# Start addresses of the linear layers' operands set to multiples of 2048 bytes

## The chip, the cores and the metric

The kernel runs on one core of one Trainium2 chip. The metric is the device time of one execution in microseconds (us), the median of several runs. TensorE does the matrix products; VectorE (DVE), ScalarE (ACT) and GpSimd (POOL) do the rest out of the same on-chip memory, SBUF; SyncE (SP) issues the transfers from DRAM. SBUF has 128 partitions; a tile takes the same byte range of each, and "start" below means the byte of a partition at which an operand begins.

## The reference

512 tokens of 1024 features go through two blocks of two layers each, in float32.

```python
def first_block(x, ...):
    h = x
    for layer in range(2):
        hn = _rmsnorm(h, norm_mix[layer])
        h = h + attention(hn) @ w_o          # layer 0: stick-breaking, layer 1: dilated with rotary
        h = h + _swiglu(_rmsnorm(h, norm_ffn[layer]), w_gate[layer], w_up[layer], w_down[layer])
    return _rmsnorm(h, norm_final)

def second_block(x, ...):
    h = x
    for layer in range(2):
        mix = hgrn2_mixer(h, ...) if layer == 0 else swa_sink_mixer(h, ...)
        h = layer_norm(ALPHA * h + mix, ...)
        ff = conv_ffn(h, ...)                # up-projection, causal convolution of 3 taps, SiLU gate, down
        h = layer_norm(ALPHA * h + ff, ...)
    return h
```

Each attention has 16 heads of 64 features, or 8 of 128 in the recurrence `hgrn2_mixer`; each feed-forward has 2816 hidden features.

## The kernel before

Activations lie with their features on the partitions and the 512 tokens along them. A float32 matrix product is carried by three products of the type float32r: each operand is split into a first part (its value rounded) and a second part (the rest), and `mm3` multiplies first by first, second by first and first by second into the same PSUM bank. The three products that recur everywhere are thus `xh` with `whi`, `xh` with `wlo`, and `xl` with `whi`; in a profile's `bank<-xh,whi` the two names are the two operands in the order of the trace, first the streamed one (moving), then the one that is loaded into the array (stationary, a weight tile of 128x128, 512 bytes of a partition).

Weights come in blocks of 512 KB (`w_dma`), are split by ScalarE (`w_hi`) and VectorE (`w_lo`) into one of three pairs of rooms `whi0/wlo0` to `whi2/wlo2` (a fourth pair from the second block on), and are used by

- `cols`: 128 output features by all 512 tokens, the weights stationary, the activations moving, 512 columns (2048 bytes) at a time. Nearly all products have this form. `cols_n`, `half_unit` and `late_unit` are variants, the last two also by halves of 256 tokens, around the second block's layer norms.
- `rows`: four tiles of tokens by 256 features for the attentions' values, with the activations stationary and the weights moving, 256 columns (1024 bytes) at a time.

The moving activations are `xh`/`xl` (normed layer input, `[128, 8, 512]`, held for the whole program in the pool `fix`), `hh`/`hl` (hidden features of a feed-forward) and `oh`/`ol` (output of an attention). The last two pairs lie in pools that are opened and closed by layer, the rows of one are 2048 bytes apart, so that all eight have the same start modulo 2048.

Four stretches are woven: the products of an attention's projections alternate by hand-written shares (`weave`) with the attention itself, whose steps wait for VectorE and ScalarE. Between them the feed-forwards run products alone. The order of all engines' instructions is the order of the Python program; no scheduler changes it.

Where a tile lies is decided by the pools alone: `fix`, `ring`, `tmp` and the layer's pool stand behind one another, and within a pool tiles stand in the order in which they are first asked for, each rounded up to 32 bytes. In `fix` the first is `vecs` with 1924 bytes, so that what follows starts off every larger multiple. The starts that come of it, modulo 2048:

| tile | used as | before | after |
|---|---|---|---|
| `x`, `xh`, `xl` | moving (and stationary in `rows`) | 544 | 0 |
| `whi0`..`wlo3`, staging `wst` | stationary (and moving in `rows`) | 1888, so 1888, 352, 864, 1376 by weight tile | 0, so 0, 512, 1024, 1536 |
| `hh`, `hl` of the first block; `oh`, `ol` of the first block | moving | 1888 | 0 |
| `hh`, `hl` and `oh`, `ol` of the second block | moving | 1504 | 0 |
| `sph`, `spl` (stick-breaking, moving) | moving | 1888 and 864 | 0 and 1024 |
| `ntri`, `nones` (stick-breaking) | stationary | 352, 864 | 512, 1024 |
| `acc`, `r_bc`, `dg` | sums and factors of the norms | 1632, 1632, 1664 | 0 |

Of the kernel before, what the change touches and what calls it, by code (L numbers as in the profile page):

```python
# [8 lines left out]
F32 = mybir.dt.float32  # L9
# [7 lines left out]
P = 128  # L17
S = 512
# [8 lines left out]
# the first two weight blocks come by halves, between the tiles of x  # L27
# [6 lines left out]
# ---------------------------------------------------------------- weight order  # L34
def plan():
    """The weight tiles in the order in which the tensor engine takes them: a
    block is (matrix, [(row tile, column tile), ...], gain vector or None)."""
    out = []
# [58 lines left out]
# ------------------------------------------------------------ per-feature rows  # L97
# [25 lines left out]
def _shape_constants():  # L123
# [6 lines left out]
    i = np.arange(P)  # L130
# [16 lines left out]
    # relative position buckets: column u stands for the distance 255 - u  # L147
# [52 lines left out]
# ------------------------------------------------------------------ the program  # L200
# [9 lines left out]
class Prog:  # L210
# [3 lines left out]
    # -- small helpers  # L214
    def defer(self, f):
        """f waits for another engine: its engine takes other work first."""
        self.pend.append(f)
# [9 lines left out]
    def warm(self, n):  # L227
        """keeps the tensor engine's clock up while it waits."""
        for _ in range(n):
            self.mm(self.bank[0][:, 0:P], self.ones, self.ones, True)  # L230
# [9 lines left out]
    # -- weight stream: DRAM -> stage -> (hi, lo) parts in float32r  # L240
# [8 lines left out]
    def w_part(self, i, c):  # L249
        """the split of a part of a block."""  # L250
        if i not in self.split:
            self.split[i] = self.rooms.pop(0)
        st, (hi, lo) = self.staged[i][:, c], self.split[i]
        self.nc.scalar.activation(out=hi[:, c], in_=st, func=AF.Copy)
        self.nc.vector.tensor_tensor(out=lo[:, c], in0=st, in1=hi[:, c].bitcast(F32), op=ALU.subtract)

    def w_gain(self, i):
        """the gains of the blocks up to the i-th."""
# [11 lines left out]
    def w_room(self, pool, n):  # L270
        """room for one more split block."""
        self.rooms.append((pool.tile([P, 1024], F32R, name=f"whi{n}", bufs=1), pool.tile([P, 1024], F32R, name=f"wlo{n}", bufs=1)))

    def w_hi(self):
        """the first parts of the next block."""
# [32 lines left out]
    def w_free(self, n=1):  # L308
        """the oldest n blocks are used."""
# [3 lines left out]
    def w_done(self, n, evac):  # L313
        """the oldest n blocks are used: evac, and the split of the blocks that take their room."""
# [7 lines left out]
    # -- products: three float32r passes carry a float32 product  # L322
# [5 lines left out]
    def cols(self, name, ks, rhs, bank, evac, grain=4, then=None):  # L328
        """bank[128 features, S] (+)= W[ks, tile].T @ act; a generator of pieces."""
# [11 lines left out]
    def cols_n(self, names, ks, rhs, banks, evacs, mid=None):  # L341
        """column tiles at once, k by k, for inputs that are still being made."""
# [10 lines left out]
    def first_cols(self, names, rhs, banks, evacs, scaled=None, ready=None, late=False):  # L353
        """a phase's first three column tiles, evacuated once r_bc is made."""
# [21 lines left out]
    def rows(self, name, lhs, banks, evac, grain=16):  # L376
        """four token tiles [128 tokens, 256 features] = act.T @ W, two of them to a bank."""
# [23 lines left out]
    def half_unit(self, blk, rhs, bank, own=False):  # L401
        """k-th products of a column tile for a half of the tokens; the halves share the bank, or own one each."""
# [51 lines left out]
    def weave(self, lin, n_lin, side, n_side, lead=0, first=0):  # L454
        """the n_lin pieces of `lin`, each with its share of the n_side pieces of `side`."""
# [13 lines left out]
    # -- scores q.k of 64 features: two passes carry the three products  # L469
    def pair_tiles(self, pool, o, p):  # L470
        """operands of a pair of heads: [k first; k second], [q first; q first] of each, and q second of both;
        a third of the pairs has them where the last pairs' outputs will be."""
# [9 lines left out]
    def pair_k(self, t, src, eng=None):  # L482
        """the parts of k: the first where its head lies, the second in the other half of the partitions."""
# [16 lines left out]
    def scores(self, out, t, h, lhs, ks, qs, start):  # L500
        """out = q.k of a head, the operand `lhs` ("k" or "q") stationary."""
# [5 lines left out]
    # -- norms  # L507
    def split_act(self, dst, j, src, gain=None):
        """dst (hi, lo)[:, j] = src * gain in two float32r parts."""
# [19 lines left out]
    def rms_prep(self, m, gain):  # L529
        """x[m] is final: its part of the mean square, and its two-part product operand."""  # L530
# [3 lines left out]
    def rsqrt(self, y, v, t):  # L534
        """y = v ** -0.5 for v > 0: a first guess from the exponent's bits, three Newton steps."""
# [12 lines left out]
    def rms_stats(self):  # L548
        """r_tok[token, tile] and r_bc[*, token] = (mean square + 1e-6) ** -0.5"""
# [16 lines left out]
    def ln_shift(self, m, banks):  # L566
        """less the mean of x[0] over its features, which a layer norm doesn't see."""
# [8 lines left out]
    def ln_add(self, m, bank, cs=slice(0, S), direct=False):  # L576
        """x[m] is complete with what `bank` adds, and enters the sums of x and of its square."""
# [18 lines left out]
    def ln_stats(self, hf):  # L596
        """the factors of the tokens of a half; a generator of its small steps."""
# [32 lines left out]
    def ln_apply(self, hf):  # L630
        """x = LN(x) of a half of the tokens, and its two-part product operand; a generator of pieces."""
# [35 lines left out]
    def layer_norm(self, units, frees, g, b, split=True, table=None):  # L667
        """the last products before a layer norm, by halves of the tokens: the norm of the first
        half goes on beside the products of the second. `frees`: units whose block is used up then."""
# [39 lines left out]
    def bridge(self, units, third, done, fill=()):  # L709
        """the first products after a layer norm, by halves of the tokens, beside the norm of the second half."""  # L710
# [67 lines left out]
    # -- set-up  # L778
    def setup(self):
# [4 lines left out]
        for i in range(3):  # L784
            self.w_room(self.ring, i)
# [4 lines left out]
        self.ident = f.tile([P, P], F32, name="ident")  # L790
        self.x = f.tile([P, KT, S], F32, name="x")
        self.xn = (f.tile([P, KT, S], F32R, name="xh"), f.tile([P, KT, S], F32R, name="xl"))
        nc.scalar.dma_start(out=self.vecs, in_=A["vecs"])
# [7 lines left out]
        self.ones = f.tile([P, P], F32, name="ones")  # L801
        nc.vector.memset(self.ones, 1.0)
        self.mean_w = f.tile([P, P], F32, name="mean_w")
        nc.vector.memset(self.mean_w, 1.0 / P)
        self.avg = f.tile([P, 2], F32, name="avg")
        nc.vector.memset(self.avg, 1.0 / 1024)
        self.eps6 = f.tile([P, 1], F32, name="eps6")
        nc.vector.memset(self.eps6, 1e-6)
        self.acc = f.tile([P, S], F32, name="acc")
        self.r_bc = f.tile([P, S], F32, name="r_bc")  # L810
        self.r_tok = f.tile([P, 4], F32, name="r_tok")
        self.dg = f.tile([P, 4, P], F32, name="dg")
        self.small = f.tile([P, 8], F32, name="small")

    def setup2(self):
        nc, f = self.nc, self.fix
        # lower bound: first row of the softmax over the two rows of logits
        self.lb = f.tile([P, 16], F32, name="lb")
        t = f.tile([P, 32], F32, name="lbt")
# [11 lines left out]
    def rel_setup(self):  # L831
        """what makes DRAM rows of every head's bias by distance: 128 equal rows each, to be read sheared."""
# [8 lines left out]
        self.hot = f.tile([33, 384], F32, name="hot")  # L841
        self.nc.vector.memset(self.rel, 1.0)
# [12 lines left out]
    # -- first block, layer 0: stick-breaking attention  # L855
    def stick(self):
        nc = self.nc
        lin, zr = Ring(self.bank[0:2] + self.bank[7:]), Ring(self.bank[2:6])
        with self.tc.tile_pool(name="stick", bufs=1) as pool:
# [74 lines left out]
            def s1b(p, u):  # L934
                W, off, banks = UW[u], UOFF[u], st[p, u]
                for h, e in enumerate(st.pop((p, u, "e"))):
# [7 lines left out]
                    # a block of keys and all later ones, for the blocks of keys before it  # L944
# [59 lines left out]
    # -- gated feed-forward of the first block  # L1004
# [43 lines left out]
    # -- first block, layer 1: dilated attention, its branches as one softmax  # L1048
    def dilated(self):
# [3 lines left out]
        with self.tc.tile_pool(name="dil", bufs=1) as pool:  # L1053
# [12 lines left out]
            def tick(n=1):  # L1066
                """what waits for a rope, some pieces later."""
# [61 lines left out]
            # block (keys j, queries i) of the weights lies at i + 3 j for the first head of a pair, 7 + 3 i + j for the second  # L1129
# [555 lines left out]
```

## Time and profile before

| | |
|---|---|
| median of 3 runs | 2611.56 us |
| lowest and highest | 2609.57, 2617.84 us |
| span of the profiled execution | 2614.2 us |
| TensorE busy | 2568.6 us (98%) |
| VectorE, ScalarE, GpSimd busy | 60%, 40%, 17% |
| granted clock of TensorE, mean | 0.988 |

The span of the profiled execution is itself 2.6 us over the median of the runs and inside their range. In the profile a matmul's duration is longer than the distance to the next one's start, since matmuls overlap in the array; where they follow one another without a wait, the distance from start to start is what one costs.

### The profile page before, as it was taken

Reading aid. Unit: us, or ns where it says so; the run is one execution under the profiler, and the core shown is the slowest. Engines: PE = TensorE matmul, PEld = TensorE weight load, DVE = VectorE, ACT = ScalarE, POOL = GpSimd, SP = SyncE. Lnnn points to the kernel's source line nnn. Section 1 sums busy time; section 2 is a strip of 40 time slices with the busy share of each in tenths; the row PEclk is TensorE's granted clock in tenths of the full one; section 3 lists DMA queues with packets and bytes.
Section 4 is the critical chain, followed back from the end, with each engine's and each line's share of the span. In section 5 each row is a group of like instructions: output and inputs, shape, how many; then the busy total and the mean of one; then the engine's idle time right before and its main releaser. Section 6 shows DMA issues by size and latency. Waiting matters only on the chain.

```text
span 2614.2 us, 32942 instructions
## 1 busy us (share of the span) xinstructions
PE 2568.6 (98%) x12732; PEld 2093.9 (80%) x12732; DVE 1556.6 (60%) x2580; ACT 1045.7 (40%) x1736; POOL 443.7 (17%) x394
## 2 busy tenths in 40 slices
PE   9999999999999999999999999999999999999998
PEld 7777888888767778888888888788788777888787
DVE  7665643444767654344476667754556788745556
ACT  6666422223445442222333333533333574523243
POOL 2111100001545210000111124100102325000103
PEclk9999999999999999999999999999999999999999
DMA  4111222222322122322221112232222312222221
GB/s 144 56 42 49 89 97 97 86 100 97 98 64 77 63 92 89 105 89 97 97 93 58 64 41 73 92 110 89 89 96 82 105 49 81 89 97 87 99 92 54
DMA packets 71277, 220.19 MB, mean 84 GB/s; under 512 B 8741, under 2 KB 15013, under 8 KB 71120
## 3 DMA queue, kind: packets, MB, share of 16 engines
q1 hardware_dynamic: 70512, 216.57, 24.3%
q8 instruction: 100, 1.64, 0.3%
q0 software_dynamic: 464, 1.27, 0.2%
q14 instruction: 57, 0.47, 0.1%
q10 hardware_dynamic: 144, 0.25, 0.0%
HBM read 209.14 MB, written 5.24 MB: 82 GB/s over the span
## 4 chain that ended last, share of the span: by engine, by line
PE 89%; DVE 8%; ACT 2%; issue 1%; DMA 0%; SPq 0%; POOL 0%; ACTq 0%; DVEq 0%
PE bank L225 88%; DVE wlo L295 1%; DVE lt L640 1%; DVE pr L1544 1%; PE bank L1161 1%; ACT whi L286 1%; DVE pr L1531 0%; DVE ln_sm L545 0%; DVE hg L1261 0%; DVE pr L1153 0%; PE bank L1554 0%; DVE xl L653 0%; DVE hq L1338 0%; DVE sm L1534 0%; DMA x<-in_xT 0%
## 5 line engine op out<-in xcount | busy, mean ns | idle before, releaser
L286 ACT ACTIVATE whi<-wst 128x1024 fp32r<-128x1024 f32 (+2 forms) x410 | 411.1, 1008 | 974.4 <-PE bank L225 781.9
L225 PE MATMUL bank<-xh,whi 128*128 128x512 f32 (+1 forms) x1992 | 788.6, 396 | 6.9 <-DVE xh L650 4.8
L225 PE MATMUL bank<-xl,whi 128*128 128x512 f32 (+1 forms) x1992 | 781.5, 392 | 4.9 <-DVE xl L653 2.6
L225 PE MATMUL bank<-xh,wlo 128*128 128x512 f32 (+1 forms) x1992 | 779.1, 391 | 1.4 <-DVE wlo L295 1.3
L295 DVE TENSOR_TENSOR wlo<-wst,whi 128x1024 fp32r<-128x1024 f32 (+2 forms) x392 | 485.3, 1243 | 100.4 <-ACT whi L286 97.4
L225 PEld LDWEIGHTS bank<-xh,whi 128*128 128x128 f32 x1992 | 378.7, 190 | 100.6 <-issue 14.7
L225 PEld LDWEIGHTS bank<-xl,whi 128*128 128x128 f32 x1992 | 378.2, 190 | 96.7 <-DVE xl L653 7.1
L225 PEld LDWEIGHTS bank<-xh,wlo 128*128 128x128 f32 x1992 | 378.8, 190 | 83.0 <-DVE wlo L295 2.3
L225 PE MATMUL bank<-hh,whi 128*128 128x512 f32 (+1 forms) x760 | 286.9, 378 | 0.0
L225 PE MATMUL bank<-hh,wlo 128*128 128x512 f32 (+1 forms) x760 | 285.9, 376 | 0.0
L225 PE MATMUL bank<-hl,whi 128*128 128x512 f32 (+1 forms) x760 | 285.6, 376 | 0.0
L527 POOL TENSOR_TENSOR acc<-acc,sq 128x512 f32<-128x512 f32 x35 | 49.9, 1427 | 803.4 <-ACT sq L526 803.0
L770 DVE TENSOR_TENSOR x<-x,bank 128x512 f32<-128x512 f32 x96 | 66.0, 688 | 190.7 <-PE bank L225 190.6
L225 PEld LDWEIGHTS bank<-hh,wlo 128*128 128x128 f32 x760 | 143.1, 188 | 27.3 <-issue 0.5
L225 PEld LDWEIGHTS bank<-hh,whi 128*128 128x128 f32 x760 | 143.0, 188 | 27.3 <-issue 0.5
L225 PEld LDWEIGHTS bank<-hl,whi 128*128 128x128 f32 x760 | 143.1, 188 | 26.8
L574 POOL TENSOR_TENSOR x<-x,r_bc 128x512 f32<-128x512 f32 x32 | 46.7, 1466 | 492.4 <-ACT r_bc L572 430.6
L225 PE MATMUL bank<-whi,xh 128*128 128x256 f32 x416 | 121.1, 291 | 0.0
L1406 DVE SCALAR_TENSOR_TENSOR b<-bank,vecs,b 128x511 f32<-128x511 f32 x88 | 65.9, 749 | 92.3 <-ACT b L1404 90.7
L1406 DVE SCALAR_TENSOR_TENSOR a<-bank,vecs,a 128x511 f32<-128x511 f32 x88 | 65.9, 749 | 90.2 <-ACT a L1404 88.7
L225 PE MATMUL bank<-whi,xl 128*128 128x256 f32 x416 | 118.3, 284 | 0.0
L225 PE MATMUL bank<-wlo,xh 128*128 128x256 f32 x416 | 118.1, 284 | 0.0
(285 smaller groups left out, 3536.6 us busy)
## 6 DMA issues: line engine op xcount, KB each, us to landing
wst<-in_w SPq DMA_DIRECT2D x314, 512.0 KB, 3.2
wst<-in_w SPq DMA_DIRECT2D x64, 448.0 KB, 3.1
wst<-in_w SPq DMA_DIRECT2D x36, 256.0 KB, 2.6
t<-t SPq DMA_DIRECT2D x56, 64.0 KB, 2.0
rel_scratch<-sq SPq DMA_DIRECT2D x16, 192.0 KB, 2.0
x<-in_xT SPq DMA_DIRECT2D x8, 256.0 KB, 6.1
bias<-rel_scratch SPq DMA_DIRECT2D x16, 128.0 KB, 2.8
out_dram<-x SPq DMA_DIRECT2D x16, 128.0 KB, 1.8
```

Source lines behind the costliest of these rows:

```text
L225: self.nc.tensor.matmul(out, lhsT=l, rhs=r, start=start, stop=True, skip_group_check=True)
L286: self.nc.scalar.activation(out=self.split[i][0][:, 0:n], in_=self.staged[i][:, 0:n], func=AF.Copy)
L295: (eng or self.lo_eng or self.nc.vector).tensor_tensor(out=lo[:, 0:n], in0=st[:, 0:n], in1=hi[:, 0:n].bitcast(F32), op=ALU.subtract)
L527: self.defer(lambda: eng.tensor_tensor(out=self.acc, in0=self.acc, in1=sq, op=ALU.add))
L574: nc.gpsimd.tensor_tensor(out=self.x[:, j, :], in0=self.x[:, j, :], in1=self.r_bc, op=ALU.subtract)
L640: nc.vector.scalar_tensor_tensor(out=t, in0=self.x[:, m, cs], scalar=gm, in1=self.acc[:, cs], op0=ALU.mult, op1=ALU.mult)
L770: self.nc.vector.tensor_tensor(out=self.x[:, m, :], in0=self.x[:, m, :], in1=bank, op=ALU.add)
L1161: nc.tensor.transpose(bk[:, P * j:P * j + P], pr[h][:, P * j:P * j + P], self.ident)
L1406: nc.vector.scalar_tensor_tensor(out=t[:, sh:S], in0=bank[:, 0:S - sh], scalar=self.vec(f"cw{l}{tap}", f), in1=t[:, sh:S], op0=ALU.mult, o ...
L1544: nc.vector.tensor_scalar(out=pr[h][:, 0:W], in0=pr[h][:, 0:W], scalar1=sm[:, 4 + h:5 + h], scalar2=None, op0=ALU.mult)
```

## The change

No instruction is added, taken away, or put elsewhere in any engine's order, and none gets another shape. Tiles get other starts: in `setup` the small tiles (`ident`, `ones`, `mean_w`, `avg`, `eps6`, `r_tok`, `small`, `lb`, `lbt`) are allocated first, then 160 bytes of padding (`pad`), which bring the pool to a multiple of 2048; behind them `x`, `xh`, `xl`, `acc`, `r_bc`, `dg` and the weight rooms, all of whole multiples of 2048 bytes. In `rel_setup` a padding of 384 bytes (`pad2`) does the same for the pool `fix2`, behind which the layers' pools of the second block begin. Everything moves up by 160 bytes or, in `fix2` and behind, by up to 544. Comments were dropped as well.

```diff
     def setup(self):
...
-        for i in range(3):
-            self.w_room(self.ring, i)
...
         self.ident = f.tile([P, P], F32, name="ident")
+        self.ones = f.tile([P, P], F32, name="ones")
+        self.mean_w = f.tile([P, P], F32, name="mean_w")
+        self.avg = f.tile([P, 2], F32, name="avg")
+        self.eps6 = f.tile([P, 1], F32, name="eps6")
+        self.r_tok = f.tile([P, 4], F32, name="r_tok")
+        self.small = f.tile([P, 8], F32, name="small")
+        self.lb = f.tile([P, 16], F32, name="lb")
+        self.lbt = f.tile([P, 32], F32, name="lbt")
+
+        f.tile([P, 40], F32, name="pad")
         self.x = f.tile([P, KT, S], F32, name="x")
         self.xn = (f.tile([P, KT, S], F32R, name="xh"), f.tile([P, KT, S], F32R, name="xl"))
+        self.acc = f.tile([P, S], F32, name="acc")
+        self.r_bc = f.tile([P, S], F32, name="r_bc")
+        self.dg = f.tile([P, 4, P], F32, name="dg")
+        for i in range(3):
+            self.w_room(self.ring, i)
...
-        self.ones = f.tile([P, P], F32, name="ones")
         nc.vector.memset(self.ones, 1.0)
-        self.mean_w = f.tile([P, P], F32, name="mean_w")
...
-        self.acc = f.tile([P, S], F32, name="acc")
-        self.r_bc = f.tile([P, S], F32, name="r_bc")
-        self.r_tok = f.tile([P, 4], F32, name="r_tok")
-        self.dg = f.tile([P, 4, P], F32, name="dg")
-        self.small = f.tile([P, 8], F32, name="small")
...
     def rel_setup(self):
...
         self.hot = f.tile([33, 384], F32, name="hot")
+        f.tile([P, 96], F32, name="pad2")
```

## Rows read from the trace of the kernel before

**Rows 1.** The page's first parts: busy us (share of span) by engine; granted clock.

```profile
span 2614.2 us, 32942 instructions
...
PE 2568.6 (98%) x12732; PEld 2093.9 (80%) x12732; DVE 1556.6 (60%) x2580; ACT 1045.7 (40%) x1736; POOL 443.7 (17%) x394
...
PEclk9999999999999999999999999999999999999999
```

**Rows 2.** The page's chain that ended last, by line.

```profile
PE bank L225 88%; DVE wlo L295 1%; DVE lt L640 1%; DVE pr L1544 1%; PE bank L1161 1%; ACT whi L286 1%; DVE pr L1531 0%; DVE ln_sm L545 0%; DVE hg L1261 0%; DVE pr L1153 0%; PE bank L1554 0%; DVE xl L653 0%; DVE hq L1338 0%; DVE sm L1534 0%; DMA x<-in_xT 0%
```

**Rows 3.** Groups by form, TensorE: names, shapes, xcount | busy us, mean ns | idle before.

```profile
L225 PE MATMUL bank<-xh,whi 128*128 128x512 f32 x1880 | 751.5, 400 | 1.3 <-ACT xh L516 0.9 <-DVE x L770 0.3
...
L225 PE MATMUL bank<-hh,whi 128*128 128x512 f32 x648 | 254.8, 393 | 0.0
...
L225 PE MATMUL bank<-whi,xh 128*128 128x256 f32 x416 | 121.1, 291 | 0.0
...
L225 PE MATMUL bank<-oh,whi 128*128 128x512 f32 x208 | 84.6, 407 | 0.1
...
L225 PE MATMUL bank<-hh,whi 128*128 128x256 f32 x112 | 32.1, 286 | 0.0
...
L225 PE MATMUL bank<-oh,whi 128*128 128x256 f32 x96 | 27.5, 286 | 0.0
```

**Rows 4.** Timeline, TensorE, 550 to 590: start us, duration us, instruction; 173 rows.

```profile
549.74 0.39 PE L225 MATMUL bank<-xl,whi 128*128 128x512 f32 x1
...
589.87 0.40 PE L225 MATMUL bank<-xh,whi 128*128 128x512 f32 x1
```

**Rows 5.** The same, 510 to 545 us, first block's feed-forward; 156 rows.

```profile
509.73 0.39 PE L225 MATMUL bank<-hh,whi 128*128 128x512 f32 x1
...
544.86 0.39 PE L225 MATMUL bank<-hl,whi 128*128 128x512 f32 x1
```

**Rows 6.** The same, 275 to 290 us, first attention's output; 68 rows.

```profile
274.67 0.39 PE L225 MATMUL bank<-ol,whi 128*128 128x512 f32 x1
...
289.86 0.39 PE L225 MATMUL bank<-oh,whi 128*128 128x512 f32 x1
```

**Rows 7.** The same, 1745 to 1785 us, second block's feed-forward; 174 rows.

```profile
1744.61 0.39 PE L225 MATMUL bank<-hh,whi 128*128 128x512 f32 x1
...
1784.81 0.40 PE L225 MATMUL bank<-hl,whi 128*128 128x512 f32 x1
```

**Rows 8.** The same, 36 to 41 us, `rows` of the first values; 45 rows.

```profile
35.80 0.28 PE L225 MATMUL bank<-whi,xh 128*128 128x256 f32 x1
...
40.98 0.28 PE L225 MATMUL bank<-wlo,xh 128*128 128x256 f32 x1
```

**Rows 9.** The same, 2005 to 2015 us, second block's halves; 86 rows.

```profile
2004.76 0.28 PE L225 MATMUL bank<-hh,whi 128*128 128x256 f32 x1
...
2014.96 0.28 PE L225 MATMUL bank<-hh,wlo 128*128 128x256 f32 x1
```

**Rows 10.** The same around 128 us: stick-breaking sums, then a projection's products.

```profile
127.73 0.40 PE L225 MATMUL bank<-sph,ntri 128*128 128x512 f32 x1
127.96 0.34 PE L225 MATMUL bank<-sph,nones 128*128 128x384 f32 x1
128.13 0.39 PE L225 MATMUL bank<-spl,ntri 128*128 128x512 f32 x1
```

**Rows 11.** The same at 1470 us: four passes of plain float32, in one row.

```profile
1470.36 1.88 PE L225 MATMUL bank<-sq,ones 128*128 128x512 f32 x4
```

**Rows 12.** One tile's instructions: name, xcount: duration ns min/median/max.

```profile
L225 PE MATMUL bank<-sq,ones x16: 590/592/685, 1401.5 to 1600.9; 128*128 128x512 f32 x16
```

**Rows 13.** Windows, the four woven stretches: us, then busy us by engine; sum.

```profile
665.00:870.00 205.00, 194.96 (x1016) 150.59 (x1015) 148.04 (x312) 90.51 (x199) 107.44 (x76) 0.96 0.25 76
...
sum 800.00, PE 776.88 PEld 632.84 DVE 566.76 ACT 393.28 POOL 239.21; mean PE 194.22 PEld 158.21 DVE 141.69 ACT 98.32 POOL 59.80
```

More of the change, by code (lines that the diff above doesn't have):

```diff
@@ L800, in setup @@
         self.load_const(self.ident, "ident")
-        self.ones = f.tile([P, P], F32, name="ones")
         nc.vector.memset(self.ones, 1.0)
-        self.mean_w = f.tile([P, P], F32, name="mean_w")
         nc.vector.memset(self.mean_w, 1.0 / P)
-        self.avg = f.tile([P, 2], F32, name="avg")
         nc.vector.memset(self.avg, 1.0 / 1024)
-        self.eps6 = f.tile([P, 1], F32, name="eps6")
         nc.vector.memset(self.eps6, 1e-6)
-        self.acc = f.tile([P, S], F32, name="acc")
-        self.r_bc = f.tile([P, S], F32, name="r_bc")
-        self.r_tok = f.tile([P, 4], F32, name="r_tok")
-        self.dg = f.tile([P, 4, P], F32, name="dg")
-        self.small = f.tile([P, 8], F32, name="small")
     def setup2(self):
-        nc, f = self.nc, self.fix
-        self.lb = f.tile([P, 16], F32, name="lb")
-        t = f.tile([P, 32], F32, name="lbt")
+        nc = self.nc
+        t = self.lbt
         l0, l1 = self.vec("lb0"), self.vec("lb1")
```

## The prediction

> **What bounds the kernel now.** I read the page's busy shares first, then the chain of waits, then the groups by form, then the timeline of single stretches. TensorE is busy 2568.6 of 2614.2 us at a granted clock of 0.9 or more in every slice [rows 1], that is, at the upper of its two levels, 2.4 GHz. 88% of the chain is the one line that issues products [rows 2]; no other line has more than 1%. So what a product costs from its start to the next one's start sets the time, and busy time alone can't tell it, because matmuls overlap: their mean is near 400 ns [rows 3], their distance is not.
>
> The distance is to be read in the timeline, as last start less first start, by the rows between them. All these products have the same shape and type, and none waits:
>
> - `xh`/`xl` moving, start 544 modulo 2048: 589.87 - 549.74 = 40.13 us over 172 steps, 0.2333 us [rows 4].
> - `hh`/`hl` of the first block, start 1888: 35.13 over 155 steps, 0.2266 us [rows 5]. `oh`/`ol` of the first block, also 1888: 15.19 over 67, 0.2267 us [rows 6].
> - `hh`/`hl` of the second block, start 1504: 40.20 over 173, 0.2324 us [rows 7].
>
> So one product costs one of three steady prices, and two unlike tiles with the same start cost the same. The clock is the same in all, and the same names (`hh`, `hl`) have two prices in two places of memory. What differs is the start. That is the ground for a change that does nothing but move starts.
>
> **What of the start matters?** The rows allow two readings. (a) The start relative to that of the weights which are loaded for the next product meanwhile. Weight tiles begin at 1888 plus multiples of 512. Modulo 512 the moving operand is then off by 0 for start 1888, by 128 for 1504, by 192 for 544, and the price rises in that order: 0.2266, 0.2324, 0.2333. After the change every pair is off by 0, as first-block `hh` is now. (b) The start itself. Then residue 0 is a place that no row shows, since every operand of these products now begins at 32 modulo 64, and it could cost anything from a column per cycle to more than now. I take (a), because it orders all three prices with one number and because after the change the distances between moving and stationary operand are exactly those of the cheapest case shown; only the common shift by 160 bytes is new. Against (a) stands one place: in the stick-breaking sums both operands have the same residue modulo 512 too, and the 512-column product there still takes 127.96 - 127.73 = 0.23 us and the one of 384 columns 0.17 [rows 10]. They alternate in length and come eight at a time, so they may never settle; this is why (a) doesn't get more than a bit over half.
>
> **The change part by part.** Nothing is added, removed or moved in any queue, so there are no waits to cost and no transfers that start elsewhere; the paddings and the gathered small tiles cost nothing by themselves, since allocation makes no instruction. All cost lies in the distance per product. Counts come from [rows 3], where each row stands for one of three equal products, so times three.
>
> 1. `xh`/`xl`, 512 columns: 3 x 1880 = 5640 products, 0.2333 - 0.2266 = 6.7 ns each: 37.6 us.
> 2. `hh`/`hl` and `oh`/`ol` at 1504. Of the 648 `hh` rows the two gated feed-forwards of the first block have 2 x 22 x 8 = 352, so the second block 296; of the 208 `oh` rows the first block has 2 x 8 x 8 = 128, the second 80. 3 x 376 = 1128 products, 0.2324 - 0.2266 = 5.7 ns: 6.5 us. The other 1440, at 1888 now, stay as they are.
> 3. `rows` with moving weights, 3 x 416 = 1248 products of 256 columns: 5.18 us over 44 steps, 0.1177 us [rows 8]. Their operands are off by 320 modulo 512. At the rate of the cheapest case, half of 0.2266, one takes 0.1133: 4.4 ns, 5.5 us.
> 4. Halves of `hh` and `oh`, 3 x (112 + 96) = 624 products: 10.20 over 85, 0.1200 us [rows 9]; to 0.1133 it is 6.7 ns, 4.2 us. No row shows 256 columns in the favoured position, so 3 and 4 are bounded by 0 and by these values; I take them, because 0.1133 is the rate of the nearest row. The `xh` halves stand among the waits of the norms; nothing is taken for them.
>
> Sum: 53.8 us.
>
> What of it lies beside other work? In the feed-forwards TensorE never waits, and VectorE and ScalarE, which split the weights, are busy 60% and 40% on the whole [rows 1], so that 3% more pace is covered. In the four woven stretches (0 to 215, 665 to 870, 1310 to 1550 and 2010 to 2150 us) TensorE is busy 776.9 of 800 us, the least in the second [rows 13]; it idles 23, and there a faster product may only make it wait for a softmax step. They hold 3 x (128 + 128 + 192 + 72) = 1560 of the products of item 1 (10.4 us) and all of item 3, 15.9 us together; I let a third be lost, 5 us. If none is, the sum is 54; if all is and 256 columns give nothing, 37.6 - 10.4 + 6.5 = 34. I take 49: 2614.2 becomes 2565. The profiled execution lies 2.6 us over the median, so the forecast for the median is 2611.6 - 49 = **2563 us**, its own range 2557 to 2578.
>
> **The rivals.**
>
> *Aligned is better than anything shown.* By reading (b) an operand that begins on a round address could stream a column per cycle: 512 at 2.4 GHz are 0.2133 us. The nearest row is the plain float32 product, whose four passes take 1.88 us [rows 11]; less the 0.59 of one pass's own duration [rows 12], three steps of 0.43, or 0.215 for half of one, so the array itself has no stall of 13 ns to pay. At 0.215 items 1 and 2 give 103 + 20, the 1440 others 17, the 256-column ones 13 + 8, in all 161; a third of the woven part lost (14): 2465 us. The Trainium skill (TensorE: Matmul & The Clock Gate, Back-to-back issue gap) puts the gap of a warm matmul at N/2.4 + 2.5 ns, which for 512 columns is an estimate of 216 ns; no product in the rows reaches it. By that figure items 1 and 2 and the 1440 others would give some 130 us. For this rival speaks that every start now is 32 modulo 64; against it, that three starts with that in common have three prices.
>
> *No effect.* Residue 0 happens to cost on average what the three cost now, (5640 x 0.2333 + 1440 x 0.2266 + 1128 x 0.2324) / 8208 = 0.2320 us, within 0.95 ns, or the price follows something that moves along with the tiles: 2612 us. The Trainium skill (SBUF — State Buffer, SBUF: two separate sides) says that TensorE has its own ports to the memory and never waits on anyone; by that rule no start would matter and this rival holds. The trace disagrees in that equal products cost 0.2266 and 0.2333.
>
> *Residue 0 is as bad as 544.* By reading (b), if the own start counts and 0 falls on the dear side, the common price is 0.2333: the 1440 products at 1888 lose 6.7 ns (9.6 us), the 1128 at 1504 lose 0.9 (1.0 us): 2622 us. It is slower as soon as the common price passes 0.2320, and each ns over that costs 8.2 us. For it: the sums of [rows 10], with equal residues, are nearer to 0.2333 than to 0.2266.
>
> **How the numbers follow.** A measurement of this kernel can tell about 0.3% (8 us) from no change. Forecast 0.55; better than shown 0.15; no effect 0.13; dear 0.17. Faster by over 0.3%: 0.70; within: 0.14; slower: 0.16. The range goes from 2540 to 2625: it holds the forecast, no effect, the dear case at 0.2333 and a small part of the better one; the rest of that (0.12) and a residue 0 that is dearer than any start shown (0.06) are left out.
>
> **What would show it.** In the timeline after, all 512-column products of the feed-forwards, `xh` and `hh`, in both blocks, stand 0.2266 us apart, and 256-column ones near 0.1133. If `xh` and `hh` agree but at another distance, (a) is wrong and the start itself counts; at 0.2133 to 0.22 the first rival holds, at 0.2333 the last. If `xh` and `hh` still differ, neither reading is right. If the distances are right and the gain is under 40 us, the woven stretches kept it, and TensorE's idle time there has grown by as much.

## The result, and the profile after

The kernel after takes 2582.87 us (median of 4 runs, 2580.42 to 2584.82), the kernel before 2614.7 us (median of 4 runs, three of them those of the table above). The ratio is 0.9879, with a 95% interval from 0.9862 to 0.9897: 1.2% faster. The forecast was 2563 us, with an own range from 2557 to 2578 us: the measured time lies above that and inside the whole range from 2540 to 2625. The gain forecast was 49 us, the gain measured 32, so the direction and the mechanism have to be judged apart from the size. And since the whole range also holds the time of no effect, 2612 us, it is the distances, and not the total alone, that have to tell which mechanism was at work.

The page of the kernel after, the lines that answer to [rows 1] and [rows 2]:

```profile
span 2582.3 us, 32942 instructions
...
PE 2533.5 (98%) x12732; PEld 2097.1 (81%) x12732; DVE 1557.3 (60%) x2580; ACT 1045.8 (40%) x1736; POOL 443.6 (17%) x394
...
PE bank L225 87%; DVE wlo L295 1%; DVE lt L640 1%; DVE pr L1548 1%; PE bank L1165 1%; ACT whi L286 1%; DVE pr L1157 0%; DVE pr L1535 0%; DVE ln_sm L545 0%; DVE hg L1265 0%; PE bank L1558 0%; DVE hq L1342 0%; DVE xl L653 0%; DMA x<-in_xT 0%; DVE sm L1538 0%
```

The number of instructions is the same, the chain runs over the same lines of the program (they have moved by four in the file), and the busy times of VectorE, ScalarE and GpSimd are within 0.7 us of those before. TensorE is shorter by 35.1 us of busy time, the span by 31.9.

The same products as in [rows 4], [rows 7], [rows 8] and [rows 9], in the timeline of the kernel after (start us, duration us, instruction; first and last, with the same number of rows between them):

```profile
542.48 0.39 PE L225 MATMUL bank<-xl,whi 128*128 128x512 f32 x1
...
581.47 0.39 PE L225 MATMUL bank<-xh,whi 128*128 128x512 f32 x1
...
1727.73 0.39 PE L225 MATMUL bank<-hh,whi 128*128 128x512 f32 x1
...
1766.95 0.39 PE L225 MATMUL bank<-hl,whi 128*128 128x512 f32 x1
```

```profile
35.76 0.28 PE L225 MATMUL bank<-whi,xh 128*128 128x256 f32 x1
...
41.04 0.28 PE L225 MATMUL bank<-wlo,xh 128*128 128x256 f32 x1
...
1980.98 0.28 PE L225 MATMUL bank<-hh,whi 128*128 128x256 f32 x1
...
1991.18 0.28 PE L225 MATMUL bank<-hh,wlo 128*128 128x256 f32 x1
```

`xh` takes 38.99 us over 172 steps, `hh` of the second block 39.22 over 173: both 0.2267, where they had 0.2333 and 0.2324. But `rows` takes 5.28 over 44, 0.1200, where it had 0.1177, and the halves 10.20 over 85, still 0.1200. The 512-column products have become what the prediction said, the 256-column ones have not.

To see where the whole difference lies, I added up the distances from each TensorE instruction's start to the next one's, by kind, over both traces. The two programs issue the same products in the same order, so the sums can be subtracted:

| kind | products | before, us | after, us | difference |
|---|---|---|---|---|
| `xh`/`xl`, 512 columns | 5640 | 1341.8 | 1313.7 | -28.1 |
| `hh`/`hl`, 512 | 1944 | 447.3 | 442.0 | -5.3 |
| `oh`/`ol`, 512 | 624 | 148.7 | 147.3 | -1.4 |
| `rows`, 256 | 1248 | 156.0 | 158.0 | +2.0 |
| halves of `hh` and `oh`, 256 | 624 | 81.6 | 81.7 | +0.1 |
| halves of `xh`, 256 | 336 | 59.4 | 61.3 | +1.9 |
| all others | 2315 | 368.2 | 367.0 | -1.2 |
| sum | | 2603.0 | 2571.1 | -31.9 |

By place: the four woven stretches together hold 799.2 us before and 798.2 after, the rest 1803.7 and 1772.9. So nearly all of the gain, 30.8 us, came outside the woven stretches, and 1.0 us in them. The windows of the kernel after over the same instructions as [rows 13] (us, then busy us of PE, PEld, DVE, ACT and POOL, granted clock, DMA share, GB/s), and then the three windows of before that [rows 13] leaves out:

```profile
0.00:214.10 214.10, 209.20 (x1110) 165.97 (x1110) 148.45 (x235) 141.17 (x262) 43.93 (x62) 1.00 0.23 76
655.60:862.00 206.40, 194.40 (x1017) 151.28 (x1015) 149.39 (x313) 90.61 (x199) 107.34 (x76) 0.96 0.25 76
1294.90:1534.10 239.20, 235.42 (x1454) 205.45 (x1454) 159.50 (x216) 78.37 (x110) 45.01 (x29) 1.00 0.20 66
1986.30:2125.90 139.60, 134.19 (x818) 111.88 (x817) 111.11 (x380) 83.34 (x215) 42.85 (x49) 0.96 0.24 75
sum 799.30, PE 773.21 PEld 634.58 DVE 568.44 ACT 393.49 POOL 239.12; mean PE 193.30 PEld 158.64 DVE 142.11 ACT 98.37 POOL 59.78
```

```profile
0.00:215.00 215.00, 210.60 (x1110) 165.74 (x1110) 148.45 (x235) 141.21 (x262) 43.94 (x62) 1.00 0.22 76
...
1310.00:1550.00 240.00, 236.78 (x1453) 204.79 (x1453) 159.30 (x216) 78.34 (x110) 44.90 (x29) 1.00 0.19 66
2010.00:2150.00 140.00, 134.54 (x818) 111.72 (x817) 110.96 (x380) 83.22 (x215) 42.94 (x49) 0.96 0.22 74
```

TensorE's idle time in them went from 800.0 - 776.9 = 23.1 to 799.3 - 773.2 = 26.1 us: 3 us of what the faster products saved there became waiting. The granted clock of the four is the same before and after (1.00, 0.96, 1.00, 0.96), so it isn't the clock that kept the rest of the gain there.

### The profile page after: what moved, and what is told of

The parts are those of the page before. It is cut to its first block, busy times and chain, and to the rows that moved or that the text cites. A ratio compares the mean times of both kernels' runs of the same rounds, so it can differ in the third digit from the quotient of the medians.

```text
span 2582.3 us, 32942 instructions
## 1 busy us (share of the span) xinstructions
PE 2533.5 (98%) x12732; PEld 2097.1 (81%) x12732; DVE 1557.3 (60%) x2580; ACT 1045.8 (40%) x1736; POOL 443.6 (17%) x394
## 4 chain that ended last, share of the span: by engine, by line
PE 88%; DVE 8%; ACT 2%; issue 1%; DMA 0%; SPq 0%; POOL 0%; DVEq 0%; ACTq 0%
PE bank L225 87%; DVE wlo L295 1%; DVE lt L640 1%; DVE pr L1548 1%; PE bank L1165 1%; ACT whi L286 1%; DVE pr L1157 0%; DVE pr L1535 0%; DVE ln_sm L545 0%; DVE hg L1265 0%; PE bank L1558 0%; DVE hq L1342 0%; DVE xl L653 0%; DMA x<-in_xT 0%; DVE sm L1538 0%
## 5 line engine op out<-in xcount | busy, mean ns | idle before, releaser
L225 PE MATMUL bank<-xl,whi 128*128 128x512 f32 (+1 forms) x1992 | 773.5, 388 | 5.0 <-DVE xl L653 2.7
L225 PE MATMUL bank<-xh,wlo 128*128 128x512 f32 (+1 forms) x1992 | 770.5, 387 | 2.3 <-DVE wlo L295 2.3
```

The costliest lines, as they stand in the source:

```text
L225: self.nc.tensor.matmul(out, lhsT=l, rhs=r, start=start, stop=True, skip_group_check=True)
```

## The experiments

The theory to be tested is reading (a): a product's price follows the distance between the starts of its two operands. Its rivals are reading (b), the moving operand's own start, and, for the part of the gain that is missing, waits in the woven stretches against something in the products themselves.

**One price list by itself** (`probe_starts`). The computation is left out; streams of 48 products run alone, the moving operand's start varied against weights at 0. The lines that issue them:

```diff
+                    for i in range(count):
+                        c = (i % nw) * P
+                        nc.tensor.matmul(bk[:, 0:cols], lhsT=w[:, c:c + P], rhs=m[:, off:off + cols], start=i == 0, stop=True,
+                                         skip_group_check=True)
```

> The whole computation is left out: the kernel loads x, makes operands of it at chosen starts and lets TensorE run streams of 48 products back to back, each stream on its own tile, whose name tells the start of the moving operand modulo 2048 (m0192b: 192) against weights w0b at 0, 512, 1024, ... Theory (a), the distance of the moving start from the weights' modulo 512 counts: m0000b, m0512b and m1024b stand 0.2267 us apart, m0128b about 0.232, m0192b 0.233, and the tiles c0032b to c0544b, whose weights are shifted by as much as they, all 0.2267. Theory (b), the own start counts: c0544b and m0544-like starts differ from c0032b although the distance is 0 in all, and c0032b is not c0064b. Of 256 columns the profile after shows 0.1200 at distance 0, that is 32 cycles of 2.4 GHz over 256 as 544 is over 512: if each product pays 32 cycles whatever its length, n384r0000b stands 0.1733 apart and n256r0000b 0.1200; if the loss is one cycle in 16, 0.170 and 0.1133. If the loss comes from the load of the next weights, the distance matters in all lengths down to 128 columns. The bfloat16 tiles h0000b to h0192b, half the bytes: no loss, 0.2133 to 0.216, at any start, if the moving bytes are what collides.

The groups of this run (`m` and four digits: 512 columns, that start in bytes; `c`: both operands shifted by it; `n` and the columns, `r` and the start: fewer columns; `h`: bfloat16; the fields of a line as in [rows 3]). The busy time of a group is 47 distances and one product's own duration, 0.39 us at 512 columns:

```profile
L297 PE MATMUL bank<-m0032b,w0b 128*128 128x512 f32 x48 | 11.4, 395 | 0.0
...
L297 PE MATMUL bank<-m0192b,w0b 128*128 128x512 f32 x48 | 11.4, 395 | 0.0
...
L297 PE MATMUL bank<-m0064b,w0b 128*128 128x512 f32 x48 | 11.2, 392 | 0.0
...
L297 PE MATMUL bank<-c0032b,v0032b 128*128 128x512 f32 x48 | 11.1, 390 | 0.0
...
L297 PE MATMUL bank<-c0544b,v0544b 128*128 128x512 f32 x48 | 11.1, 389 | 0.0
L297 PE MATMUL bank<-m0256b,w0b 128*128 128x512 f32 x48 | 11.0, 389 | 0.0
L297 PE MATMUL bank<-m0000b,w0b 128*128 128x512 f32 x48 | 11.0, 389 | 0.0
...
L297 PE MATMUL bank<-h0192b,u0b 128*128 128x512 bf16 x48 | 10.5, 379 | 0.0
...
L297 PE MATMUL bank<-n384r0000b,w0b 128*128 128x384 f32 x48 | 8.5, 335 | 0.0
...
L297 PE MATMUL bank<-n256r0000b,w0b 128*128 128x256 f32 x48 | 5.9, 283 | 0.0
...
L297 PE MATMUL bank<-n256r0192b,w0b 128*128 128x256 f32 x48 | 5.6, 277 | 0.0
...
L297 PE MATMUL bank<-n128r0000b,w0b 128*128 128x128 f32 x48 | 5.5, 273 | 0.0
```

Once settled, the distances in ns by start are:

| start of the moving operand, weights at 0 | 512 columns | 256 columns |
|---|---|---|
| 0, 256 (512 columns: also 512, 1024) | 226.7 | 120.0 |
| 64, 320 | 228.9 | 117.8 |
| 128, 384 | 233.3, 232.3 | 118.7 |
| 192, 448 | 233.3 | 117.8, at 192 also 113.3 |
| 32, 96, 160, 224, 288 | 233.3 to 234.2 | 117.8 to 120.0 |
| 4, 16 | 236.7, 231.7 | not tried |
| both operands at 32, 64, 160 or 544 | 226.7 | not tried |

(The 256-column values at 32, 96, 160, 224, 256, 288, 384 and 448, and the 117.8 of 192, come from `probe_mixed` below.) Reading (a) holds, with a period of 256 bytes. By (b) the moving operand's start would set the price; but at start 32 it costs 233.4 ns against weights at 0 (`m0032b`) and 226.7 against weights at 32 (`c0032b`), and `c0544b` costs the same as `c0032b`. At 512 columns distance 0 is the cheapest. At 256 columns it is the dearest, with 96: 120.0 ns are 288 cycles of 2.4 GHz and 226.7 are 544, which is 256 + 32 and 512 + 32. With 384 columns it is 173.3 ns, 416 cycles, again 32 more. So distance 0 costs 32 cycles a product above a column per cycle at these three lengths, and not a rate. At 128 columns the list ends: all five starts that were tried cost 111.6 to 111.8 ns, 268 cycles, and the distance no longer shows. With 384 columns it shows little, 173.3 at 0, 64 and 320, 174.7 at 192 and 176.0 at 128.

**The whole kernel with all operands moved off the round addresses** (`shift_544`).

```diff
-        f.tile([P, 40], F32, name="pad")
+        f.tile([P, 176], F32, name="pad")
```

> The change with its first padding 544 bytes longer, so that every operand of the linear layers begins at 544 modulo 2048, the start that xh had before, with all distances between operands as after. Theory (a), the distance to the weights counts: 0.2267 us per 512-column product everywhere and the time of after, 2583, within 0.3%. Theory (b), the own start counts: 0.2333 everywhere, 6.7 ns on 8208 products, 55 us over after, about 2637, slower than before.

Measured: 2579.83 us (2571.68 to 2581.45), ratio 0.9861 (0.9841 to 0.9881). With every operand at 544 modulo 2048, the residue that `xh` had in the kernel before, `xh` in the feed-forward stands as in the kernel after, 38.99 us over 172 steps:

```profile
542.21 0.39 PE L225 MATMUL bank<-xl,whi 128*128 128x512 f32 x1
...
581.20 0.39 PE L225 MATMUL bank<-xh,whi 128*128 128x512 f32 x1
```

Reading (b) wanted 2637 and is out. A multiple of 2048 bytes has no worth of its own.

**The change without its second padding** (`setup_only`).

```diff
-        f.tile([P, 96], F32, name="pad2")
```

> The change without its second padding: first block as after, and in the second block the feed-forward's and attention's operands begin at 1664, 128 off modulo 512, as they were off by 128 before, with the weights and xh at 0. Theory (a): their 512-column products (1128) stand 0.232 us apart, xh's stay at 0.2267 in both blocks; the time is 6 us over after, about 2589. Theory (b), the own start counts: 1664 is a new start whose price is open; if only round starts are cheap, the 1128 products at 0.2333, 2590, but then the shifted kernel loses everything.

Measured: 2582.4 us (2579.15 to 2585.67), ratio 0.9873 (0.9854 to 0.9892); I had expected some 6 us more than the kernel after, and the total doesn't show it. The trace does: `hh` of the second block, now at distance 128, takes 40.37 us over 173 steps, 0.2333, and all 512-column products of `hh` 447.6 us against 442.0.

```profile
1725.18 0.39 PE L225 MATMUL bank<-hh,whi 128*128 128x512 f32 x1
...
1765.55 0.40 PE L225 MATMUL bank<-hl,whi 128*128 128x512 f32 x1
```

Single executions of one kernel differ by up to 10 us and are mostly longer where the mean granted clock is lower: this kernel's four spans are 2583.7 and 2583.8 us at 0.988 and 2577.2 and 2577.3 at 0.990, those of the kernel after 2582.9 at 0.986, 2582.3 and 2579.6 at 0.987 and 2578.5 at 0.988. At 0.988, the one clock that both have, the difference is 5.2 us, but that is one execution against two. The two profiled executions show where the total went: `hh` and `oh` cost 6.2 us more here, but `xh`, whose places are the same in both, 3.2 us less, and the second woven stretch took 204.3 us at a granted clock of 0.97 instead of 206.4 at 0.96. For the total, then, this run is inconclusive; for the price of the products it is not.

**What follows a product of another kind** (`probe_mixed`). For the missing part of the gain: streams of 96 products with another product after every twelve (`side[3]` is 12).

```diff
+                    for i in range(count):
+                        if side and i and i % side[3] == 0:
+                            nc.tensor.matmul(bs[:, 0:side[2]], lhsT=side[1][:, 0:P], rhs=side[0], start=True, stop=True, skip_group_check=True)
+                        c = (i % nw) * P
+                        nc.tensor.matmul(bk[:, 0:cols], lhsT=w[:, c:c + P], rhs=m[:, off:off + cols], start=i == 0, stop=True,
+                                         skip_group_check=True)
```

> The whole computation is left out; streams of products alone. Part one: 16 streams of 48 float32r products of 256 columns, weights at a multiple of 512 bytes, the moving operand's start at 0, 32, ..., 480 bytes mod 512. If the distance of the starts counts modulo 256, as the 512-column streams had it in the first probe, starts r and r+256 read alike, 0 and 256 stand at 120.0 ns, 192 and 448 at 113.3 ns and 64 and 320 at 117.8 ns; if the period is 512, 448 reads otherwise than 192. Part two: streams of 96 products of 512 columns with one other product after every twelve, at distance 0 and at distance 192, the other one being 128 columns at distance 0 or 64, 256 columns at distance 0, 512 columns at distance 192, or a plain float32 product of 128 columns. Settling theory (in the woven stretches of the kernel after, the first ten or so products behind another kind stand at 227 to 236 ns and only then at 226.7): at distance 0 the first 4 to 10 products behind each other product read 228 to 236, the mean of twelve 228 to 231, and at distance 192 the mean of twelve stays at 233 whatever stands between, so the gain of a product is 2 to 5 ns instead of 6.7. Rival theory (the woven loss comes of waits and the other engines' traffic, not of the change of kind): at distance 0 the products behind the other one read 226.7 at once, a gain of 6.7 for all twelve.

Timeline of the stream at distance 0 with a 256-column product between (the twelve are merged into one row):

```profile
243.18 0.28 PE L283 MATMUL bank<-s256b,w0b 128*128 128x256 f32 x1
243.29 2.91 PE L285 MATMUL bank<-d0s256b,w0b 128*128 128x512 f32 x12
246.04 0.28 PE L283 MATMUL bank<-s256b,w0b 128*128 128x256 f32 x1
```

and at distance 192:

```profile
266.05 0.28 PE L283 MATMUL bank<-s256b,w0b 128*128 128x256 f32 x1
266.16 2.96 PE L285 MATMUL bank<-d192s256b,w0b 128*128 128x512 f32 x12
268.96 0.28 PE L283 MATMUL bank<-s256b,w0b 128*128 128x256 f32 x1
```

A round is 2.86 us against 2.91. In the trace the twelve distances at distance 0 read 233, 235, 229, 232, 231, 227 ns and then 226.7, again and again; at distance 192 they are 233.3 throughout. Behind a plain float32 product of 128 columns it takes ten distances until 227 stands. So the good price has to be won back after each interruption, over five to ten products, and twelve products gain 53 ns instead of 80: the settling theory holds, the rival (226.7 at once) falls. One guess missed: at distance 192 a 256-column product read 113.3 ns in the first probe and 117.8 here. Both are steady for dozens of products, so there are two settled states; what decides between them isn't shown (`rooms_192` below has both in one execution).

**Another way to distance 0, and away from it.** Three kernels in which each weight tile is 64 columns longer, so that the weights can begin at another column. They differ from each other in that column alone. Against the kernel after, three small tiles and the paddings are placed otherwise too, such that every other operand still begins at a multiple of 256 bytes.

```diff
-        self.rooms.append((pool.tile([P, 1024], F32R, name=f"whi{n}", bufs=1), pool.tile([P, 1024], F32R, name=f"wlo{n}", bufs=1)))
+        self.rooms.append((pool.tile([P, 1088], F32R, name=f"whi{n}", bufs=1), pool.tile([P, 1088], F32R, name=f"wlo{n}", bufs=1)))
...
+    def w_take(self, i):
+        self.held[i] = self.rooms.pop(0)
+        o = START.get(i, START0)
+        self.split[i] = tuple(t[:, o:o + 1024] for t in self.held[i])
```

`rooms_0` has `START0 = 0`, `rooms_64` has 16, and `rooms_192` has 48 for the weights of `rows`, 16 for those that meet halves of the tokens, and 0 for all others (columns of 4 bytes).

> The kernel after with every weight tile made 64 columns (256 bytes) longer, its products still at the tile's first column: the weight tiles of the ring now begin at 0, 256, 512 and so on of 2048 bytes, all other operands at a multiple of 256. No instruction is added or moved. If the distance of the two starts counts modulo 256 bytes, every product stands as in the kernel after: 226.7 ns at 512 columns, 120.0 at 256, and the time is that of after, 2579 to 2586 us. If it counted modulo 512 or 2048, half of the weight tiles would stand at another distance and the time would be 10 to 25 us longer.

> As rooms_0, but all weights begin at column 16 of their tile, 64 bytes further; the start of every x, h and o operand is what it is in rooms_0. By the distance theory the products of 512 columns stand at a distance of -64 bytes (192 modulo 256), where the probes read 233.3 ns instead of 226.7: some 6500 products in steady streams times 6.6 ns, 43 us, and about 4 us from the products behind another kind, less 2.5 us of the 256-column products of rows() (117.8 instead of 120.0) and 2 to 5 us of the halves: 2583 + 41 = 2624 us (2616 to 2631), longer than the kernel before, since there the products of h and o of the first block stood at 226.7. By the theory that a moving operand's own start is what counts, 2583 us, as rooms_0.

> As rooms_0, but the weights that rows() moves begin at column 48 (192 bytes) of their tile and those that stand still against halves of the tokens at column 16 (64 bytes), so that all 256-column products have a distance of 192 modulo 256, while all 512-column products keep 0. The probes read two steady distances for 256 columns there, 113.3 and 117.8 ns, against 120.0 at 0: some 1150 steady products of rows() and 790 of halves gain 2.2 to 6.7 ns each, 4 to 13 us: 2570 to 2579 us, against rooms_0 at 2583. If the halves' gain is lost to the norms beside them, 1.7 to 5 us less of it: 2575 to 2580.

Measured:

| kernel | median, us | ratio to before | interval |
|---|---|---|---|
| `rooms_0` | 2584.30 (2579.43 to 2586.84) | 0.9875 | 0.9862 to 0.9888 |
| `rooms_64` | 2623.84 (2618.63 to 2626.23) | 1.0027 | 1.0015 to 1.0039 |
| `rooms_192` | 2574.85 (2570.78 to 2576.40) | 0.9835 | 0.9822 to 0.9849 |

`rooms_0` is the kernel after, though its weight tiles begin at odd multiples of 256 as well: the period is 256 bytes in the whole kernel too. `rooms_64` moves nothing but the weights, by 64 bytes, and falls behind the kernel before, as forecast from the price list (2624). Its `xh` and its second-block `hh`, the same places as above, stand 0.2333 apart (40.14 us over 172 steps, 40.36 over 173):

```profile
553.36 0.39 PE L227 MATMUL bank<-xl,whi 128*128 128x512 f32 x1
...
593.50 0.39 PE L227 MATMUL bank<-xh,whi 128*128 128x512 f32 x1
...
1756.43 0.39 PE L227 MATMUL bank<-hh,whi 128*128 128x512 f32 x1
...
1796.79 0.40 PE L227 MATMUL bank<-hl,whi 128*128 128x512 f32 x1
```

`rooms_192` gives each length of product the distance that suits it, and has the lowest time and the lowest ratio of the kernels here. Against `rooms_0`, by the sums of distances, `rows` took 154.2 us instead of 158.6, the halves of `xh` 58.4 instead of 61.5, those of `hh` and `oh` 80.4 instead of 81.7: 8.8 us, and the medians differ by 9.5. In its timeline both pairs of rows stand 0.118 apart (5.19 over 44, 10.01 over 85), which is the poorer of the two settled states; elsewhere in its `rows`, later in the first woven stretch, the 113.3 occurs, and the mean of those beyond the tenth that don't wait is 116.2.

```profile
35.08 0.28 PE L228 MATMUL bank<-whi,xh 128*128 128x256 f32 x1
...
40.27 0.28 PE L228 MATMUL bank<-wlo,xh 128*128 128x256 f32 x1
...
1975.23 0.28 PE L228 MATMUL bank<-hh,whi 128*128 128x256 f32 x1
...
1985.24 0.28 PE L228 MATMUL bank<-hh,wlo 128*128 128x256 f32 x1
```

**Which weights does the distance refer to?** Pairs of operands in turn (`probe_pairs`).

```diff
+                    for i in range(count):
+                        m, w = pairs[i % len(pairs)]
+                        c = (i % 8) * P
+                        nc.tensor.matmul(banks[k % 8], lhsT=w[:, c:c + P], rhs=m, start=i == 0, stop=True, skip_group_check=True)
```

> The whole computation is left out; streams of 96 float32r products of 512 columns alone, their moving operand at 0 or 192 (in two streams at 64 or 160) bytes modulo 256 and the weight tiles likewise, in turn. It tells whether the distance is taken from the weights that a product uses or from those that are loaded meanwhile for the next product. Streams of one pair, as a base: 0 with 0 at 226.7 ns, 192 with 0 at 233.3, 192 with 192 at 226.7. Own-weights theory: pairs (0 with 0, 192 with 192) in turn 226.7 ns, pairs (0 with 192, 192 with 0) in turn 233.3. Next-weights theory, which is the one that the prediction put into words: (0 with 0, 192 with 192) in turn 233.3, since each is streamed while the weights of the other are loaded, and (0 with 192, 192 with 0) 226.7. The same for 64 and 160. One moving tile with weights at 0 and 192 in turn, and moving tiles at 0 and 192 in turn with weights at 0: between the two, about 230, by either theory. Third theory (neither: what counts is how the starts follow one another on each side): the two alternating streams of pairs cost the same.

Measured, steady means: (0 with 0, 192 with 192) in turn 231.6 ns, (0 with 192, 192 with 0) 233.3; (64 with 64, 160 with 160) 234.0, (64 with 160, 160 with 64) 230.0; the moving operand alone in turn 226.7, the weights alone in turn 230.0. No theory gives this list: own weights wanted 226.7 for the first and the third, next weights 226.7 for the second and the fourth, and the third theory the same for both of a pair. What can be relied on is a distance that stays the same through a stream; how mixed ones add up stays open.

## Why the prediction was right, and where not

**What bounds the kernel.** Right: the distance from start to start of the products alone moved, and the span followed it.

**Reading (a).** Right, and for the reason given: `xh` and `hh` agree in both blocks at the price of [rows 5]. The modulus was too large, 256 instead of 512, which changes nothing here, and the words that tied it to the next product's weights have no support in the pairs in turn. The doubt drawn from [rows 10] fits the settling: products that come eight at a time and change length each time have no run in which to reach the steady price. No run here has such a stream by itself, so this stays an inference.

**Term 1, 37.6 us: measured 28.1.** The price was right. Outside the woven stretches 3910 products that stand beyond the tenth after a change of kind gained 6.67 ns each, 26.1 us, and those nearer to one 1.0. In the woven stretches the prediction counted 1560 products, 10.4 us; between the same instructions the traces have 1500. Of these the 565 beyond the tenth gained 6.3 ns each (3.6 us), the 736 nearer only 3.1 (2.3 us), since a step of the attention interrupts them, and the 77 that are the last before such a step 0.3 us in all. The timeline behind such a step, in the kernel after:

```profile
60.72 0.28 PE L225 MATMUL bank<-spl,nones 128*128 128x256 f32 x1
60.84 0.39 PE L225 MATMUL bank<-xh,whi 128*128 128x512 f32 x1
61.07 0.40 PE L225 MATMUL bank<-xh,wlo 128*128 128x512 f32 x1
...
62.00 0.39 PE L225 MATMUL bank<-xl,whi 128*128 128x512 f32 x1
62.22 0.39 PE L225 MATMUL bank<-xh,whi 128*128 128x512 f32 x1
...
63.13 0.39 PE L225 MATMUL bank<-xh,wlo 128*128 128x512 f32 x1
```

The first five steps take 1.16 us, 0.232 each, the last four 0.91, 0.2275. The rest of the term, 122 products that wait in one of the two traces, lost 5.1 us. TensorE's other products in the same stretches became shorter by 1.7, so part of the loss may only have passed from one kind to the other. The second woven stretch, the dilated attention, gained nothing at all: it takes 205.1 us before, 206.4 after, 206.0 in `rooms_192` and 207.0 in `rooms_64`, where a product is dearer, all at a granted clock of 0.96. It takes 207.6 in `rooms_0`, at 0.95, and 204.3 in `setup_only` and 198.7 in `shift_544`, both at 0.97. These seven executions go with the clock and not with the product's price, which is the same in five of them. Whether the clock makes the stretch longer there, or longer waits in it lower the clock, the traces don't tell.

**The third that is lost in the woven stretches, 5 us.** Too small: of 15.9 us forecast there without it, 1.0 came. The 14.9 missing are 7.3 of `rows` (5.5 forecast, 1.8 lost), 4.3 of the products of `xh` that gained less, most of it by the settling, and 5.1 of those that waited, less 1.7 that the side work gained. The prediction saw only the waits. The test that it set, that the idle time there would have grown by as much as was missing, failed as well: it grew by 3 us.

**Term 2, 6.5 us: measured 6.7.** Right, `hh` 5.3 and `oh` 1.4.

**Terms 3 and 4, 5.5 and 4.2 us: measured a loss of 2.0, and 0.1.** This is the step that failed: half of the 512-column price was taken for 256 columns. The prediction scaled the price of 512 columns to 256 by length, though [rows 9] showed 0.1200 for halves of the very tiles whose whole products cost 0.2324 in [rows 7]: half the columns, more than half the price. The price is a column per cycle plus a term that distance 0 brings to 32 cycles at 256, 384 and 512 columns alike, and 32 cycles weigh twice as much on half the columns. The bound below nothing was missing: at distance 0 the 256-column products cost what they do at their worst, and `rows` left a better place, 320, for it. For the halves the list isn't exact: they cost 0.1200 in [rows 9], off by 128, where the probe read 118.7 ns. The halves of `xh`, for which nothing was taken, lost 1.9 us, half of it in products that wait in one of the traces.

The sum came to 54 us before any allowance, and 32 were measured. Of the 22 missing these two terms account for 11.8, term 1 for 9.5, nearly all of it in the woven stretches, and the halves of `xh` for 1.9; other products gained 1.2. The 5 us that were allowed for covered part of it, so that the forecast itself was 17 us off.

**The rivals.** *Better than shown* fell: no start, of seventeen, gave a float32r product of 512 columns less than 226.7 ns. The Trainium skill's 216 ns (TensorE: Matmul & The Clock Gate, Back-to-back issue gap) is met by bfloat16 streams, at 215.8 and at all five starts tried, not by float32r. *No effect* fell, since equal products cost 226.7 or 233.3 ns by their operands' places. The Trainium skill says (SBUF — State Buffer, SBUF: two separate sides) that TensorE never waits on anyone. What the prediction drew from it, that no start matters, doesn't hold for float32r. The sentence itself isn't touched by that: from 30 to 300 us of `probe_starts` VectorE, ScalarE and GpSimd are busy 0.00 us, and the prices differ all the same, so they are no wait for another engine. *As bad as 544* fell with reading (b). The price that it would have had, 2622 us, is that of `rooms_64`, reached by distance.

## What to carry to other kernels

Where a stream of products bounds a kernel, read the distance from start to start by shape and by place, and compare equal products: a difference at equal clock points to the operands' places, and 64 bytes of the weights' start were worth 1.5% here (`rooms_64` against `rooms_0`). For float32r let the moving and the stationary operand begin at the same byte modulo 256 where products have 512 columns and run long, and let the moving one begin 192 bytes further, modulo 256, where they have 256; the address itself doesn't matter. Don't scale a price by length before two lengths at the same place have been seen, and don't count a steady price for products that are interrupted every ten.

## What the runs showed of the hardware

- The distance of two float32r products depends on their operands' starts modulo 256 bytes: 512 columns cost 544 cycles at 0 and 560 at 32, 96, 128 and 192, 256 columns 288 at 0 and 272 to 283 at 192; 128 columns cost 268 at every start tried. Four bytes off are the worst that was seen, 236.7 ns (568 cycles). bfloat16 shows none of it, 215.8 ns at starts 0 to 192. What in the chip makes the distance count stays open.
- In most streams five to ten products passed after another kind before the price stood, and a stream can settle in two states at one distance (113.3 or 117.8 ns).
- One moving tile at 0 and one at 192 in turn, against weights at 0, cost 226.7 ns, the price of distance 0 alone. Why is open.
- Executions of one kernel differ by up to 10 us with the mean granted clock (0.985 to 0.990), which limits what a total can tell; sums of distances by kind told differences of a few us where totals could not.
